# Moving two 32-byte scale tiles from the left to the right end of SBUF in an fp32 encoder-layer kernel

## The chip, the cores and the metric

The kernel runs on one core of a Trainium2 chip. The metric is the device time of one execution in microseconds (us), the median of three runs. Everything said of durations comes from one profiled execution of the kernel before the change.

## The reference

The computation is one layer of a hybrid encoder over two sequences of 1024 tokens with 1024 features each, everything in fp32, and a last normalisation. Cut to what matters:

```python
def layer(x, c, ...):
    mod = silu(c) @ w_ada + b_ada
    sh1, sc1, ga1, sh2, sc2, ga2 = split(mod, 6)
    h = rmsnorm(x, g_mix) * (1.0 + sc1) + sh1
    z = h @ w_in                                  # q_lat 256, kv_lat 128, k_pe 64, f_in 512
    y_mla = mla_group(...)                        # 4 heads, keys 128 + 64 rotary, values 128, softmax
    y_four = fourier_group(f_in, w_four)          # real part of a 2-D FFT over (sequence, 64 channels)
    x = x + ga1 * (concat([y_mla, y_four]) @ w_out)
    h2 = rmsnorm(x, g_ffn) * (1.0 + sc2) + sh2
    return x + ga2 * ((silu(h2 @ w_gate) * (h2 @ w_up)) @ w_down)     # FFN width 2816
# both sequences: y = rmsnorm(layer(x, c), g_final)
```

The two "scale tiles" of the change are `s1`: for each sequence, `g_mix * (1 + sc1)`, the per-feature factor of the first normalisation, as a tile of 128 partitions by 8 floats (32 bytes per partition).

## The kernel before

Every large product is done with three TensorE matmuls in place of one. A helper, `split` (L63 and L64), cuts an fp32 tile into a rounded high part (`fp32r`, ScalarE, L63) and the low rest (VectorE or GpSimd, L64). A helper, `mm3` (L79 to L81), then adds high x high, high x low and low x high into one PSUM bank. So a matmul of the profile at L79, L80 or L81 can belong to any stage; its tile names tell which. After the arrow stands the moving operand first and then the stationary one (`bank<-H,wh`: `H` moves, `wh` stays); `128*128 128x512` means a stationary operand of 128 columns and a moving operand of 512 columns. Loading the stationary operand is an instruction of its own (LDWEIGHTS, engine `PEld`).

The stages, in order of time:

- Modulation vectors, folding of weights and input transposes (about the first 100 us): weights arrive from HBM and PE works on them as they land.
- Input projection and first half of the Fourier mixing (`wz_h`, `wz_l`: 448 columns; `wcs_h`, `wcs_l`: 280 columns for the cosine part, 256 for the sine part; the stationary operands are the tokens, `eoh` and `eol`). In this stage there are 24 special matmuls in a row whose stationary operand `zoc` has only 4 columns.
- Second half of the Fourier mixing (`tb`, `wm`), attention (`ps_s`, `ppt`, `pt`, `gb`, `wv`), and 128-column transposes against an identity (`ident`, `identr`).
- The FFN, from 740 us to the end. Its products are done by a recursive block scheme on 512-column tiles: `H` holds blocks of the normalised input or of the second product, `wh` and `wl` are the split parts of weights or intermediate blocks, and intermediate blocks go through HBM scratch (`s_d`, `t_d`).

All order of work is fixed in the program; the queues of each engine run it as written.

The memory of a partition is filled from two ends. Pools opened without an option stack from the left (low addresses), pools with `side="right"` from the right (high addresses). The pools at the left begin with `const`, which holds, in this order, `ident` and `identr` (512 bytes each), `mhalf`, `cmask`, and eight tiles of 32 bytes: `s1` (two), `sh1`, `s2`, `sh2`. The right stack begins with a pool `edge` whose only tile before the change is one of 104 floats that nothing reads:

```python
edge = ctx.enter_context(tc.tile_pool(name="edge", bufs=1, side="right"))   # L86
edge.tile([P, 104], F32, name="edge")                                        # L87
```

In front of the right pools, another unused tile (`gapz`, 120 floats) makes the pool `zp` a whole multiple of 512 bytes long.

Of the kernel before, what the change touches and what calls it, by code (L numbers as in the profile page):

```python
# [12 lines left out]
F32 = mybir.dt.float32  # L13
# [8 lines left out]
P = 128  # L22
D = 1024
N = 1024
NC = D // P
# [28 lines left out]
def hybrid_encoder_kernel(ctx: ExitStack, tc: tile.TileContext, a: dict):  # L54
# [28 lines left out]
    const = ctx.enter_context(tc.tile_pool(name="const", bufs=1))  # L83
    tiny = ctx.enter_context(tc.tile_pool(name="tiny", bufs=4))
    dram = ctx.enter_context(tc.tile_pool(name="dram", bufs=1, space=DRAM))
    edge = ctx.enter_context(tc.tile_pool(name="edge", bufs=1, side="right"))  # L86
# [37 lines left out]
        nc.vector.tensor_tensor(out=r, in0=w, in1=y, op=ALU.mult)  # L124
        return r

    s1 = [const.tile([P, NC], F32, name=f"s1_{s}") for s in range(2)]
    sh1 = [const.tile([P, NC], F32, name=f"sh1_{s}") for s in range(2)]
    s2 = [const.tile([P, NC], F32, name=f"s2_{s}") for s in range(2)]
    sh2 = [const.tile([P, NC], F32, name=f"sh2_{s}") for s in range(2)]  # L130
# [1097 lines left out]
    with ExitStack() as st:  # L1228
# [117 lines left out]
        for k in range(nit + 4):  # L1346
# [9 lines left out]
            if k < nit:  # L1356
                s, b, h, u = items[k]
# [14 lines left out]
            if 0 <= k - 2 < nit and (k - 2) % 4 == 3:  # L1372
                s, b, h, u = items[k - 2]
# [668 lines left out]
```

## Time and profile before

| what | value |
|---|---|
| time, median of 3 runs | 2016.65 us (2015.29, 2016.65, 2016.70) |
| the profiled execution: its own time, and its span | 2015.8 us, 2015.8 us |
| mean granted TensorE clock | 0.995 |
| PE busy | 1973.1 us, 98% |
| weight loads (PEld) busy, beside PE | 1620.0 us, 80% |
| VectorE (DVE), ScalarE (ACT), GpSimd (POOL) busy | 1390.5, 889.0 and 849.8 us |
| DMA, mean rate over the span | 187 GB/s |

The profile has one row per group of alike instructions: line, engine, operation, output tile, input tiles, shape, count, then busy time and mean duration, then idle time before them with what ended it. Matmuls are pipelined: each is shown as lasting until its last result is out, so neighbours overlap, and what a matmul costs in a stream is the distance from its start to the next one's start, not its duration. That distance is read from the view in order of time, or from a window in which PE never idles: length divided by count.

### The profile page before, as it was taken

The numbers are of one execution on the slowest core, as the hardware profiler recorded it, in microseconds if no ns is written. First come the engines' busy times: TensorE is split into PE (matmuls) and PEld (weight loads), VectorE is DVE, ScalarE is ACT, GpSimd is POOL, SyncE is SP. The second block draws the span as 40 slices with busy tenths as digits, with TensorE's granted clock in tenths as the row PEclk, the third lists the DMA queues.
The fourth block names the chain that finished last, engine by engine and source line by source line (L and its number), as shares of the span: only waits on it lengthen the run. The fifth ranks groups of instructions, "written<-read, shape, count | busy, mean of one in ns | idle before, by whom it ended". The sixth has DMA issues, their size and how long they took to land.

```text
span 2015.8 us, 27568 instructions
## 1 busy us (share of the span) xinstructions
PE 1973.1 (98%) x9526; PEld 1620.0 (80%) x9526; DVE 1390.5 (69%) x2064; ACT 889.0 (44%) x1720; POOL 849.8 (42%) x1012
## 2 busy tenths in 40 slices
PE   6899999999999999999999999999999999999998
PEld 3778778888888877888888888888888888888886
DVE  4557757766687678777777567788755655656784
ACT  2665535555565563333333356453333333335541
POOL 0654312111223237779779410344644554420152
PEclk8999999999999999999999999999999999999999
DMA  9785884445553575645646597665333333267762
GB/s 385 262 318 193 283 331 114 122 94 121 150 123 105 188 256 197 205 158 198 202 155 202 176 314 230 230 229 185 126 99 100 107 103 105 99 203 242 251 228 86
DMA packets 179449, 376.59 MB, mean 187 GB/s; under 512 B 17996, under 2 KB 57548, under 8 KB 175468
## 3 DMA queue, kind: packets, MB, share of 16 engines
q1 hardware_dynamic: 156908, 305.60, 45.3%
q0 software_dynamic: 21824, 68.17, 11.3%
q8 instruction: 75, 1.23, 0.2%
q10 hardware_dynamic: 576, 1.05, 0.1%
q14 instruction: 66, 0.54, 0.1%
HBM read 262.75 MB, written 120.39 MB: 190 GB/s over the span
## 4 chain that ended last, share of the span: by engine, by line
PE 59%; DVE 2%; issue 1%; POOL 1%; ACT 0%; POOLq 0%; DVEq 0%; ACTq 0%
PE bank L80 20%; PE bank L79 20%; PE bank L81 20%; DVE wl L64 1%; DVE val L152 0%; DVE val L1834 0%; DVE H L64 0%; DVE val L1806 0%; POOL rs_y L107 0%; DVE val L149 0%; POOL out_dram L1840 0%; DVE val L1722 0%; POOL rs_w L109 0%; POOL rs_w L110 0%; DVE val L1708 0%
## 5 line engine op out<-in xcount | busy, mean ns | idle before, releaser
L79 PE MATMUL bank<-H,wh 128*128 128x512 f32 x1232 | 480.8, 390 | 3.0 <-DVE val L152 1.3
L80 PE MATMUL bank<-H,wh 128*128 128x512 f32 x1232 | 480.0, 390 | 0.3 <-DVE H L64 0.3
L81 PE MATMUL bank<-H,wl 128*128 128x512 f32 x1232 | 479.8, 390 | 0.2 <-DVE wl L64 0.2
L79 PEld LDWEIGHTS bank<-H,wh 128*128 128x128 f32 x1232 | 231.4, 188 | 53.7 <-DVE val L152 2.6
L64 DVE TENSOR_TENSOR wl<-draw,wh 128x512 fp32r<-128x512 f32 x286 | 208.1, 764 | 90.9 <-ACT wh L63 90.2
L80 PEld LDWEIGHTS bank<-H,wh 128*128 128x128 f32 x1232 | 231.4, 188 | 48.4 <-DVE H L64 0.6
L81 PEld LDWEIGHTS bank<-H,wl 128*128 128x128 f32 x1232 | 231.4, 188 | 48.3 <-DVE wl L64 0.5
L152 DVE TENSOR_TENSOR val<-bank,val 128x512 f32<-128x512 f32 x200 | 136.6, 689 | 162.9 <-PE bank L81 162.3
L63 ACT CAST wh<-draw 128x512 fp32r<-128x512 f32 x286 | 165.1, 619 | 174.2 <-PE bank L80 129.4
L152 POOL TENSOR_TENSOR val<-val 128x512 f32<-128x512 f32 x58 | 81.0, 1398 | 344.2 <-DVE val L1806 164.5
L80 PE MATMUL bank<-wl,wh 128*128 128x512 f32 x572 | 223.3, 390 | 0.9 <-DVE wl L64 0.9
L81 PE MATMUL bank<-wh,wl 128*128 128x512 f32 x572 | 222.8, 390 | 0.0
L79 PE MATMUL bank<-wh 128*128 128x512 f32 x572 | 222.8, 389 | 0.0
L63 ACT CAST wh<-rgu 128x512 fp32r<-128x512 f32 x172 | 107.0, 622 | 257.4 <-PE bank L80 202.7
L63 ACT CAST wh<-val 128x512 fp32r<-128x512 f32 x133 | 82.2, 621 | 262.1 <-PE bank L80 244.9
L64 DVE TENSOR_TENSOR wl<-val,wh 128x512 fp32r<-128x512 f32 x133 | 125.7, 947 | 66.7 <-ACT wh L63 66.7
L64 DVE TENSOR_TENSOR wl<-rgu,wh 128x512 fp32r<-128x512 f32 x172 | 165.4, 961 | 1.4 <-ACT wh L63 1.4
L149 POOL TENSOR_TENSOR val<-rgu 128x512 f32<-128x512 f32 x80 | 107.8, 1347 | 79.4 <-DMA rgu<-in_wgu_dram 75.7
L80 PEld LDWEIGHTS bank<-wl,wh 128*128 128x128 f32 x572 | 107.5, 188 | 24.7 <-DVE wl L64 2.6
L79 PEld LDWEIGHTS bank<-wh 128*128 128x128 f32 x572 | 107.4, 188 | 22.5
L81 PEld LDWEIGHTS bank<-wh,wl 128*128 128x128 f32 x572 | 107.4, 188 | 21.9
L149 POOL TENSOR_TENSOR val<-val 128x512 f32<-128x512 f32 x89 | 119.3, 1358 | 1.3
(400 smaller groups left out, 3897.8 us busy)
## 6 DMA issues: line engine op xcount, KB each, us to landing
rgu<-in_wgu_dram SPq DMA_DIRECT2D x86, 512.0 KB, 4.0
draw<-s_d SPq DMA_DIRECT2D x143, 256.0 KB, 3.3
s_d<-val POOLq DMA_DIRECT2D x88, 256.0 KB, 3.2
draw<-t_d SPq DMA_DIRECT2D x88, 256.0 KB, 4.4
s_d<-val SPq DMA_DIRECT2D x66, 256.0 KB, 3.7
draw<-in_w_down_dram SPq DMA_DIRECT2D x55, 256.0 KB, 4.0
wada<-in_w_ada_dram SPq DMA_DIRECT2D x11, 1024.0 KB, 9.3
xt<-in_x_dram SPq DMA_DIRECT2D x16, 512.0 KB, 10.8
```

Of the source, the lines that this page charges most:

```text
L63: here["a"] = nc.scalar.copy(hi, src).ins
L64: here["v"] = (eng or nc.vector).tensor_tensor(out=lo, in0=src, in1=rd(hi), op=ALU.subtract).ins
L79: nc.tensor.matmul(out, lh, rh, start=first, stop=False, skip_group_check=cont)
L80: nc.tensor.matmul(out, lh, rl, start=False, stop=False, skip_group_check=cont)
L81: here["t"] = nc.tensor.matmul(out, ll, rh, start=False, stop=last, skip_group_check=cont).ins
L149: return eng.tensor_tensor(out=out, in0=x, in1=y, op=ALU.subtract).ins
L152: eng.tensor_tensor(out=out, in0=x, in1=y, op=ALU.add)
```

## The change

`s1` is allocated in the pool `edge` at the right end and not in `const` at the left:

```diff
@@ -124,7 +124,7 @@
-    s1 = [const.tile([P, NC], F32, name=f"s1_{s}") for s in range(2)]
+    s1 = [edge.tile([P, NC], F32, name=f"s1_{s}") for s in range(2)]
     sh1 = [const.tile([P, NC], F32, name=f"sh1_{s}") for s in range(2)]
     s2 = [const.tile([P, NC], F32, name=f"s2_{s}") for s in range(2)]
     sh2 = [const.tile([P, NC], F32, name=f"sh2_{s}") for s in range(2)]
```

The built programs have the same instructions in the same order with the same waits on every engine and queue. What differs is where tiles lie (byte addresses in a partition):

| tile | before | after |
|---|---|---|
| `ident`, `identr`, `mhalf`, `cmask` | 8320, 8832, 9344, 9376 | unchanged |
| `s1_0`, `s1_1` | 9408, 9440 | 229280, 229312 |
| every other tile, left or right | x | x - 64 |

So the distance between any two tiles is kept, except to `s1` and to the four tiles in the first row. Of the 9366 matmul instructions of the program (160 of them, plain fp32, appear twice in the trace, which makes its 9526), by the start address of the operands modulo 512:

| moving operand | stationary operand | matmuls | after |
|---|---|---|---|
| 64 | 64 | 7512 | 0 and 0 |
| 128 (`ident`, `identr`) | 64 | 776 | 128 and 0 |
| 64 | 320 | 236 | 0 and 256 |
| 320 | 320 | 204 | 256 and 256 |
| other pairs, most with a moving operand at some multiple of 32 | | 638 | each 64 less, `ident` and `identr` excepted |

The moving operands at multiples of 32 are those of the Fourier stage: a row of `wcs_h` or `wcs_l` is 536 floats (2144 bytes) long, so that from one of its eight rows (one for each 128 input features) to the next the start moves on by 96 bytes modulo 512, and `wcs_l` lies 256 from `wcs_h`.

## The prediction

> **What bounds the kernel now.** I read the page first, its busy line, its slices and its costliest groups, to see whether one engine is the limit everywhere.
>
> ```profile
> span 2015.8 us, 27568 instructions
> PE 1973.1 (98%) x9526; PEld 1620.0 (80%) x9526; DVE 1390.5 (69%) x2064; ACT 889.0 (44%) x1720; POOL 849.8 (42%) x1012
> PE   6899999999999999999999999999999999999998
> PEclk8999999999999999999999999999999999999999
> ...
> L79 PE MATMUL bank<-H,wh 128*128 128x512 f32 x1232 | 480.8, 390 | 3.0 <-DVE val L152 1.3
> ...
> L80 PE MATMUL bank<-wl,wh 128*128 128x512 f32 x572 | 223.3, 390 | 0.9 <-DVE wl L64 0.9
> ```
>
> PE is full in all but the first slices and the granted clock is at 90% or more from the second slice on (1.00 in the windows below). The two quoted groups stand three times each (L79, L80, L81): 3 x 1232 + 3 x 572 = 5,412 matmuls of 512 columns, with idle time before them of 3.0 us or less per group. So only two things can move the time much: what one matmul costs in the stream, and the few waits. The windows give the first.
>
> ```profile
> core 0: us, PE busy (x), PEclk, DMA share, GB/s
> 1414.00:1957.00 543.00, 543.00 (x2397) 1.00 0.46 151
> 930.00:1320.00 390.00, 390.00 (x1722) 1.00 0.64 213
> ```
>
> In both windows PE never idles and all matmuls have 512 columns. Take one or two off the counts for those cut by the edges: 543/2395.5 = 226.7 ns from start to start. All of these have both operands at 64 modulo 512.
>
> **The change, part by part.** Nothing is added or removed: the order of work, the waits and the queues are kept, and what changes is 64 bytes of start address. The cost is therefore a question of whether a start at 64 costs something that a start at 0 does not.
>
> *Moving operand.* The matmuls at 512 columns are all at 64, so they can't tell. The Fourier stage can, because there the start moves on by 96 bytes from row to row, and in one place the stationary operand has only 4 columns (`zoc`), so its loading is no limit:
>
> ```profile
> start us, us, engine line op out<-in xcount [idle before <-releaser]
> 176.03 0.30 PE L79 MATMUL bank<-wcs_h,zoc 128*4 128x280 f32 x1
> 176.17 0.29 PE L80 MATMUL bank<-wcs_l,zoc 128*4 128x280 f32 x1
> 176.29 0.29 PE L81 MATMUL bank<-wcs_h,zoc 128*4 128x280 f32 x1
> 176.42 0.30 PE L79 MATMUL bank<-wcs_h,zoc 128*4 128x280 f32 x1
> ...
> 176.81 0.30 PE L79 MATMUL bank<-wcs_h,zoc 128*4 128x280 f32 x1
> ...
> 177.20 0.30 PE L79 MATMUL bank<-wcs_h,zoc 128*4 128x280 f32 x1
> ...
> 177.59 0.30 PE L79 MATMUL bank<-wcs_h,zoc 128*4 128x280 f32 x1
> ...
> 177.98 0.30 PE L79 MATMUL bank<-wcs_h,zoc 128*4 128x280 f32 x1
> ...
> 178.37 0.30 PE L79 MATMUL bank<-wcs_h,zoc 128*4 128x280 f32 x1
> ```
>
> Each group of three starts 0.39 us after the one before: 176.03, 176.42, 176.81, 177.20, 177.59, 177.98, 178.37. By the layout, the moving operands of these six groups begin at 160, 256, 352, 448, 32 and 128 modulo 512 (the middle matmul of each at 256 more, so 0 is among them: the second group is 256, 0, 256). Starts at 0, 128 and 256 are as dear as starts at 32 or 96. Per matmul that is 2.34/18 = 130.0 ns. Between 280 and 512 columns the slope is (226.7 - 130.0)/232 = 0.4168 ns a column, which leaves 226.7 - 213.4 = 13.3 ns at either length that don't depend on columns. Since the `zoc` rows carry the same 13.3 ns at every start, I don't read it as a price of the start. I take 0 for the moving operand. The rows are exact to 0.01 us a group, so at most 0.01/3 = 3 ns a matmul; both signs are open.
>
> *Stationary operand.* Where 512 columns stream, the load lies under the matmul before:
>
> ```profile
> 1500.13 0.39 PE L79 MATMUL bank<-H,wh 128*128 128x512 f32 x1
> 1500.36 0.39 PE L80 MATMUL bank<-H,wh 128*128 128x512 f32 x1
> 1500.58 0.39 PE L81 MATMUL bank<-H,wl 128*128 128x512 f32 x1
> 1500.13 0.19 PEld L80 LDWEIGHTS bank<-H,wh 128*128 128x128 f32 x1
> 1500.36 0.19 PEld L81 LDWEIGHTS bank<-H,wl 128*128 128x128 f32 x1
> ```
>
> The load for L80 begins with the matmul L79 at 1500.13 and takes 0.19 us; its own matmul starts at 1500.36, so 0.04 us are spare. A shorter load is worth 0 there; one longer by over 0.04 us (a fifth) would show. Where fewer columns stream, load and stream are both near the limit, and there the trace does show something:
>
> ```profile
> 137.69 0.28 PE L79 MATMUL bank<-wcs_h,eoh 128*128 128x256 f32 x1
> 138.03 0.28 PE L79 MATMUL bank<-wcs_h,eoh 128*128 128x256 f32 x1
> 138.38 0.28 PE L79 MATMUL bank<-wcs_h,eoh 128*128 128x256 f32 x1
> 138.74 0.36 PE L79 MATMUL bank<-wz_h,eoh 128*128 128x448 f32 x1
> ```
>
> The group that begins at 137.69 has its moving operands at 128, 384, 128 and takes 0.34 us; the next two (224, 480, 224 and 320, 64, 320) take 0.35 and 0.36, so 15 ns a group or 5 ns a matmul more. The stationary operand is at 320 in all three. After the change two of the eight rows are again at multiples of 128, others than now, so for these matmuls gain and loss cancel: 0, or up to 24 groups x 15 ns = 0.4 us either way.
>
> *Transposes.* `ident` stays, its partner moves, so their distance changes.
>
> ```profile
> L1271 PE MATMUL ppt<-ident,p 128*128 128x128 f32 x512 | 69.0, 275 | 1.5 <-DVE nb L1252 0.6 <-DVE p L1258 0.3
> L352 PE MATMUL bank<-c,wf 128*128 128x128 f32 x64 | 7.8, 278 | 0.0
> L424 PE MATMUL bank<-ident,xt 128*128 128x128 f32 x32 | 5.1, 322 | 0.0
> ```
>
> The nearest rows with another distance are the 128-column matmuls of `c` and `wf` (both operands moved alike, 278 against 275 ns). So 3 ns x 776 = 2.3 us either way; I take 0, and keep the 322 ns of L424 for the rival below.
>
> *Transfers.* Every SBUF end of a DMA moves by 64 bytes too. Only the start of the kernel waits for DMA:
>
> ```profile
> PE bank L233 <- DMA wide<-in_w_ada_dram: 5.6, 3, 2.5
> PE bank L254 <- DMA wuqT<-in_wuqT_dram: 4.9, 1, 4.9
> PE bank L233 <- DMA wada<-in_w_ada_dram: 3.3, 4, 1.4
> PE bank L269 <- DMA wide<-in_w_out_dram: 2.3, 1, 2.3
> PE bank L1096 <- DMA wada<-in_w_ada_dram: 1.9, 1, 1.9
> 30.00:40.00 10.00, 5.83 (x36) 2.94 (x36) 3.38 (x8) 5.04 (x13) 1.69 (x6) 1.00 1.02 417
> ```
>
> These waits add up to 18.0 us, and in the window from 30 to 40 us the queues are full (share 1.02, 417 GB/s). Their going altogether is the far bound of a gain; nothing in the rows says that a 64-byte shift touches them, so I take 0. The Trainium skill, DMA: Bandwidth & Descriptors, section "How a descriptor splits into AXI transactions", says that a descriptor off a 256-byte boundary also fetches the bytes back to that boundary, in beats of 32 bytes. For rows of 2048 bytes at 64 that would be 66 beats where 64 suffice, an estimate of 3% or 1.5 us on a saturated stretch of some 50 us; no run here shows it, and the sum stands without it.
>
> *Other engines.* DVE, ACT and POOL are at 69% or less; their operands move alike and their cover is the PE stream. Taken as 0. `s1` is read as a per-partition scalar wherever it lies: 0.
>
> **Sum.** 2015.8 + 0 = 2015.8 us for the profiled execution, whose own time is its span. The median of the three runs, 2016.65, is 0.85 us above it; the forecast is put between the two, 2016.3. A change under 0.2% (4 us) can't be told from none here. Its own range, by 2.3 us (transposes), 0.4 us (Fourier rows) and a little from the transfers, is 2012 to 2020.
>
> **The rivals.**
>
> *All of the 13.3 ns is the start address.* Then the 5,412 matmuls above and the 1,732 others of 512 columns (20 groups of which the first and the last are quoted) lose it.
>
> ```profile
> L1242 PE MATMUL ps_s<-lat,qa 128*128 128x512 f32 x128 | 53.6, 419 | 0.7 <-ACT qa L63 0.7
> ...
> L81 PE MATMUL bank<-wm,B 128*128 128x512 f32 x32 | 12.3, 389 | 0.0
> ```
>
> 7,144 x 13.3 ns = 95 us, giving 1921. For it: 64 bytes are 16 floats, and the excess has the size of a few dozen columns. Against it: the `zoc` groups, which pay it at 0 too. The Trainium skill, TensorE: Matmul & The Clock Gate, section "Wait — 56ns, not 53.3ns?", gives N/2.4 + 2.5 ns for back-to-back matmuls, 215.8 ns at 512 columns. The trace has 226.7, so by that rule 10.9 ns a matmul are foreign to it, an estimate of 78 us or 1938 if the address were the cause. Chance 0.06.
>
> *Load and stream disturb each other less from 0.* In the `wcs` rows with 128 stationary columns the group at multiples of 128 was 5 ns a matmul cheaper. If that depends on where the moving operand lies, and not on its distance to the stationary one (which the change keeps), 512-column matmuls gain up to the same: 7,144 x 5 ns = 36 us, 1980; at half of it 1998, at 1 ns 2009. Against it: at 512 columns the load has 0.04 us to spare and the distance of 226.7 ns is the same in both windows. Chance 0.15.
>
> *The transposes get worse* (slower than before). `ident` keeps 128 while its partners go to 0. If the new distance is a bad one, each of 776 transposes pays: by the dearest row, L424, up to 322 - 275 = 47 ns, or 36 us (2053); at 10 ns 2024. It decides beyond 0.2% from 4/776 us = 5 ns each. Against it: in the rows the kind of operand changes with the distance, and L424 lies at the start, where PE waits. A loss of 1 ns on each 512-column matmul (7 us, 2023) I count here. Chance 0.11.
>
> **How the numbers follow.** The forecast has 0.68, of which 0.04 may spill over to faster (transfers) and 0.01 to slower. Faster: 0.06 + 0.15 + 0.04 = 0.25; slower: 0.11 + 0.01 = 0.12; same: 0.63. For 8 in 10 the range takes the forecast's own 2012 to 2020 and reaches to the half-sized gain (1998) and to a loss of 10 ns a transpose (2024); outside are the full gains and the large losses, some 0.17.
>
> **What would show it.** The window from 1414 to 1957 us again with 2397 matmuls or one or two beside (right), or with 2450 and more (5 ns each) or 2540 (13.3 ns each); the `zoc` groups at 0.39 us; L1271 at 275 ns; the waits for DMA at about 18 us. The prediction is wrong if the distance between 512-column matmuls changes by more than 0.5 ns, or if the first 100 us change by more than 4 us.

## The result and the profile after

The changed kernel takes 2012.44 us (median of 20 runs, 2010.8 to 2015.8), the kernel before 2016.76 us (20 runs) beside it. The ratio is 0.998, with a 95% interval of 0.9974 to 0.9987: faster by 4.3 us (2.6 to 5.2 by the interval), right at the 0.2% that I had called the bound of what can be told. All ratios below are against the kernel before on the same chip; a ratio need not be the quotient of the two medians.

The page of the profiled execution of the kernel after (span 2014.0 us, at the upper end of its runs), with the lines that answer to those of the kernel before:

```profile
span 2014.0 us, 27568 instructions
PE 1974.3 (98%) x9526; PEld 1619.1 (80%) x9526; DVE 1392.1 (69%) x2064; ACT 889.1 (44%) x1720; POOL 852.5 (42%) x1012
PE   7899999999999999999999999999999999999998
...
L79 PE MATMUL bank<-H,wh 128*128 128x512 f32 x1232 | 480.7, 390 | 3.2 <-DVE val L152 1.4
```

Its windows in the FFN, with the same columns as before, then three rows of the `zoc` matmuls in order of time, and the transposes in the view by shape:

```profile
1414.00:1957.00 543.00, 542.63 (x2395) 1.00 0.46 151
...
172.77 0.29 PE L79 MATMUL bank<-wcs_h,zoc 128*4 128x280 f32 x1
...
173.16 0.30 PE L79 MATMUL bank<-wcs_h,zoc 128*4 128x280 f32 x1
...
173.55 0.30 PE L79 MATMUL bank<-wcs_h,zoc 128*4 128x280 f32 x1
...
L1271 PE MATMUL ppt<-ident,p 128*128 128x128 f32 x512 | 69.0, 274 | 1.4 <-DVE nb L1252 0.6
```

These matmuls cost the same within a nanosecond: 542.63/2393.5 = 226.7 ns from one 512-column matmul to the next, 0.39 us a `zoc` group (172.77, 173.16, 173.55), 274 ns a transpose against 275. What differs is PE's waiting for transfers:

```profile
PE bank L254 <- DMA wuqT<-in_wuqT_dram: 4.7, 1, 4.7
PE bank L233 <- DMA wide<-in_w_ada_dram: 4.0, 2, 2.4
...
PE bank L233 <- DMA wada<-in_w_ada_dram: 2.2, 2, 1.2
...
PE bank L1096 <- DMA wada<-in_w_ada_dram: 1.7, 1, 1.7
```

These add up to 12.6 us, against 18.0 before. And where the queues are full, they move more. The window from 10 to 50 us, first of the kernel before, then of the kernel after (the columns after the engines are granted clock, DMA share and GB/s):

```profile
10.00:50.00 40.00, 29.78 (x160) 15.75 (x158) 19.14 (x47) 11.67 (x33) 1.74 (x6) 0.87 1.02 413
```

```profile
10.00:50.00 40.00, 32.65 (x163) 16.42 (x158) 18.87 (x47) 11.66 (x33) 1.73 (x6) 0.87 1.02 420
```

The share is 1.02 in both, so the queues are full in both; 420 GB/s against 413 is 1.7% more.

### The profile page after: what moved, and what is told of

It is laid out like the page before. It is cut to its first block, busy times and chain, and to the rows that moved or that the text cites. A ratio compares the mean times of both kernels' runs of the same rounds, so it can differ in the third digit from the quotient of the medians.

```text
span 2014.0 us, 27568 instructions
## 1 busy us (share of the span) xinstructions
PE 1974.3 (98%) x9526; PEld 1619.1 (80%) x9526; DVE 1392.1 (69%) x2064; ACT 889.1 (44%) x1720; POOL 852.5 (42%) x1012
## 4 chain that ended last, share of the span: by engine, by line
PE 57%; DVE 3%; issue 1%; POOL 1%; DMA 1%; ACT 0%; SPq 0%; POOLq 0%; DVEq 0%; ACTq 0%
PE bank L80 19%; PE bank L79 19%; PE bank L81 19%; DVE wl L64 1%; DMA draw<-s_d 1%; DVE val L152 0%; DVE val L1806 0%; DVE val L1834 0%; DVE val L1725 0%; DVE H L64 0%; POOL rs_y L107 0%; ACT wh L63 0%; DVE val L149 0%; POOL out_dram L1840 0%; DVE val L1708 0%
## 5 line engine op out<-in xcount | busy, mean ns | idle before, releaser
L64 DVE TENSOR_TENSOR wl<-val,wh 128x512 fp32r<-128x512 f32 x133 | 131.0, 987 | 67.4 <-ACT wh L63 67.4
```

The lines of the kernel that those rows point to most:

```text
L64: here["v"] = (eng or nc.vector).tensor_tensor(out=lo, in0=src, in1=rd(hi), op=ALU.subtract).ins
```

## Experiments

The theory after the result, T: the gain is in the transfers, because every SBUF end of a DMA now begins on a 256-byte boundary. Its rivals: P, some matmuls got cheaper; L, the place of `s1` itself counts; F, the gain lies in the FFN's transfers and not in those of the start; D (for the kernels with unlike ends), the distance between moving and stationary operand sets what a matmul costs. All kernels compute the same; only the place of tiles differs, by the edits shown, each against the kernel before.

**The change once more** (no edit to the changed kernel):

> The changed kernel once more, all operands and transfer ends at 0 modulo 512. Theory T (the gain is in the transfers at the start, because every SBUF end of a DMA now begins on a 256-byte boundary): 2012 us against 2016.7 before; in the windows from 10 to 60 us the five rates add up to about 2066 GB/s against 2024 in the trace of before; the waits of PE for DMA are some 3 to 5 us shorter; 512-column matmuls stay at 226.7 ns. Theory P (some matmuls got cheaper): the first 110 us are as before and the gain is spread over the stream. Theory N (chance of the runs): 2016.

Measured: 2012.39 us, ratio 0.9978 (0.9968 to 0.9989). The rates from 10 to 60 us are 414, 428, 423, 414 and 385 GB/s, 2064 in sum; 226.8 ns a matmul (542.5/2392.5; the counts of records vary by a few, so 226.7 to 227.0 is one value). PE's waits for DMA are shorter than in the first trace of before by 4.8 us:

```profile
PE bank L254 <- DMA wuqT<-in_wuqT_dram: 4.7, 1, 4.7
PE bank L233 <- DMA wide<-in_w_ada_dram: 4.0, 3, 2.7
PE bank L233 <- DMA wada<-in_w_ada_dram: 2.4, 2, 1.4
PE bank L269 <- DMA wide<-in_w_out_dram: 2.1, 1, 2.1
```

The effect is there again, so N falls; and P with it, since the 512-column matmuls, most of the stream, are no cheaper.

**Another pair of tiles moved:**

```diff
-    s2 = [const.tile([P, NC], F32, name=f"s2_{s}") for s in range(2)]
+    s2 = [edge.tile([P, NC], F32, name=f"s2_{s}") for s in range(2)]
```

> The s2 tiles move to the right end in place of s1, so that the same pools lie at 0 and s1 stays at the left. Theory T and theory P: the same as the changed kernel, 2012 us. Theory L (it is the place of s1 itself, read as a scalar by other engines, that counts): 2016.7 us as before.

Measured: 2013.48 us, ratio 0.9979 (0.9968 to 0.9991). L falls: `s1` is back at the left and the gain is there all the same.

**Left pools at 0, right pools at 64:**

```diff
-    edge.tile([P, 104], F32, name="edge")
+    edge.tile([P, 88], F32, name="edge")
...
-    s1 = [const.tile([P, NC], F32, name=f"s1_{s}") for s in range(2)]
+    s1 = [edge.tile([P, NC], F32, name=f"s1_{s}") for s in range(2)]
```

> The left pools lie at 0 and the right pools at 64, so 585 of the DMA's SBUF ends are on a 256-byte boundary and 486 are not, and the two operands of over 4,000 matmuls lie 64 bytes apart modulo 512. The large loads of the start (x tiles, the modulation weights) are among those at 64. Theory T: between the two kernels, 2014 to 2016.5 us, and the PE stream at 226.7 ns. Theory D (the distance between moving and stationary operand sets what a matmul costs): the windows from 930 to 1320 and from 1414 to 1957 us show another distance than 226.7 ns, by 1 to 5 ns, so 2018 to 2035 us (or as much faster).

Measured: 2039.55 us, ratio 1.0112 (1.0093 to 1.0132), slower than both and beyond what either theory had allowed. The transfers at the start were hardly hurt (419 GB/s from 10 to 50 us, 14.8 us of waits for DMA). The window in the FFN, the groups by shape from 1420 to 1950 us, and the first and the last of ten neighbours in order of time:

```profile
1414.00:1957.00 543.00, 542.50 (x2341) 1.00 0.43 143
...
L80 PE MATMUL bank<-H,wh 128*128 128x512 f32 x569 | 225.0, 395 | 0.0
...
L79 PE MATMUL bank<-wh 128*128 128x512 f32 x194 | 75.5, 389 | 0.0
...
1499.80 0.39 PE L80 MATMUL bank<-H,wh 128*128 128x512 f32 x1
...
1501.90 0.40 PE L80 MATMUL bank<-H,wh 128*128 128x512 f32 x1
```

PE is hardly idle, yet 542.5/2339.5 = 231.9 ns a matmul. The groups with `H` at the left and `wh` at the right last 395 ns, and (1501.90 - 1499.80)/9 = 233 ns lie from one of them to the next; those with both operands at the right last 389 as ever. The instructions, their order and their waits are those of before, and neither 0 nor 64 is dear when both operands share it, so this is the distance: D holds. As a check, the 3 x 1232 matmuls of `H` times 6.6 ns make 24 us, and the kernel is 23 us slower than before.

**All at 192:**

```diff
-    edge.tile([P, 104], F32, name="edge")
+    edge.tile([P, 72], F32, name="edge")
...
+    const.tile([P, 32], F32, name="shift")
```

> All pools lie at 192 modulo 512: no transfer begins on a 256-byte boundary, and it begins further from one than before (64). Theory T with a price that grows with the distance to the boundary below: slower than before, about 2019 to 2021 us, with the rates from 10 to 60 us some 6% under those of before (about 1910 GB/s in sum). That growing price is what the Trainium skill, DMA: Bandwidth & Descriptors, section 'How a descriptor splits into AXI transactions', would give: 70 beats for 2048 bytes at 192, 66 at 64, 64 at 0. Theory T with one price for every start off a boundary: 2016.7 us as before, 2024 GB/s. Theory P with the absolute address: some other time, with another distance between matmuls.

Measured: 2016.48 us, ratio 0.9997 (0.9985 to 1.0008), 226.8 ns a matmul, and in the full queues the rate of before:

```profile
10.00:50.00 40.00, 31.35 (x161) 16.14 (x156) 18.81 (x47) 11.43 (x32) 1.73 (x6) 0.87 1.02 413
```

So a start at 192 is no dearer than one at 64: one price for every start off a boundary. The growing price, as worked out from that section of the Trainium skill, isn't seen here.

**Only the pool p1 at 0, and only the pool p1 at 64.** The first has `s1` in `edge` with a tile of 88 floats, and before the first left pool after p1:

```diff
+    back = ctx.enter_context(tc.tile_pool(name="back", bufs=1))
+    back.tile([P, 16], F32, name="back")
```

> Only the pool p1, the left pool of the first 300 us, lies at 0 modulo 512; all right pools, and all left pools after it, lie at 64 as before. Of the first 26.1 MB that are loaded, 13.7 MB then land on 256-byte boundaries. In the first runs the rates of the windows from 10 to 50 us were those of the changed kernel when just the left pools were at 0 (414, 427, 424, 412 GB/s). Theory T (the transfers of the start): most of the gain, 2013 to 2014.5 us, same rates. Theory F (the transfers of the FFN, which is back at 64 here): 2016.5 us, whatever the rates at the start. The stationary and moving operands of the FFN are both at 64, so 226.7 ns.

The second has `s1` in `edge` with 104 floats, and before the pool p1, closed with it:

```diff
+        off = st.enter_context(tc.tile_pool(name="off", bufs=1))
+        off.tile([P, 16], F32, name="off")
```

> The reverse: only the pool p1 lies at 64 as before, everything else at 0. Theory T: most of the gain gone, 2014.5 to 2016.5 us, rates from 10 to 50 us as before (410, 419, 417, 404). Theory F: the whole gain, 2012.4 us.

Measured, on another chip, where the kernel before took 2018.53 us: 2014.55 us, ratio 0.9982 (0.9974 to 0.9991), and 2014.54 us, ratio 0.9985 (0.9975 to 0.9994). F in its pure form falls, since with the FFN at 64 most of the gain is there. But T, as I had put it, expected the second to lose most of the gain, and it kept over half. Its rates weren't those of before either: 416, 422, 419 and 417 GB/s from 10 to 50 us, 1674 in sum, as high as with p1 alone at 0 (413, 427, 424, 411; 1675). The other 12.4 of the first 26.1 MB, and all later transfers, were on boundaries there. Either half keeps a large part of the gain; the intervals overlap too far to say which is larger. The rates also don't fit a simple price for each transfer off a boundary: with about half of the bytes on one, the sum should lie midway between 1650 and 1679, and it lies at the upper end in both kernels. Why is open.

**All at 256, and left at 0 with right at 256.** The edits are those for 192, with 56 and 48 floats in place of 72 and 32, and those for the right at 64, with 40 floats in place of 88.

> All pools lie at 256 modulo 512. Theory T with a boundary of 256 bytes: the changed kernel's time, 2012.4 us, and its rates (415, 429, 423, 412, 387 GB/s). If the boundary were 512 bytes: 2016.5 us and the rates of before.

> Left pools at 0, right pools at 256: all transfers on 256-byte boundaries, but moving and stationary operand of most FFN matmuls 256 bytes apart. With 64 bytes apart the FFN matmuls had cost 230 to 236 ns in place of 226.7 and the kernel 2039.6 us. Theory D with a period of 256 bytes: 226.7 ns, 2012.4 us. Theory D with a period of 512 or more: another distance between matmuls in the window from 1414 to 1957 us, up to 236 ns (2040 us) or under 226.7 ns (faster than both kernels).

Measured: 2013.57 us, ratio 0.9972 (0.9962 to 0.9983), and 2013.25 us, ratio 0.9973 (0.9963 to 0.9983); rates of 415, 428, 424, 412, 386 and of 416, 428, 421, 415, 374 GB/s; 226.9 ns a matmul in both. A boundary of 256 bytes is as good as 512, and a distance of 256 as good as none. Neither can be told from the changed kernel.

**All at 128, and left at 0 with right at 128.** The edits are those for 192, with 88 and 16 floats in place of 72 and 32, and those for the right at 64, with 72 floats in place of 88.

> All pools at 128 modulo 512. Theory T with a boundary of 256 bytes: the time of before, 2016 to 2018 us, ratio 0.999 to 1.001, rates from 10 to 50 us 1650 in sum. With a boundary of 128 bytes: the changed kernel's, ratio near 0.9975, rates 1679. Moving and stationary operands coincide modulo 256, so 226.7 ns a matmul either way; the transposes now have identity and partner at the same place.

> Left pools at 0, right pools at 128: moving and stationary operand of most FFN matmuls 128 bytes apart. At 64 apart a matmul had cost 230 to 236 ns, at 256 apart 226.7 as at 0. Theory D with a period of 128: 226.7 ns, and 2013 to 2017 us by the transfers. With a period of 256: another distance, 228 to 240 ns and 2025 to 2060 us, or below 226.7 and faster than both kernels.

Measured: 2018.01 us beside 2018.31 of the kernel before, ratio 1.0003 (0.9994 to 1.0013), with the rate of before; and 2038.96 us, ratio 1.0101 (1.0086 to 1.0115). The windows of the two:

```profile
10.00:50.00 40.00, 29.58 (x164) 15.08 (x161) 19.05 (x48) 12.69 (x35) 2.28 (x7) 0.91 1.02 413
```

```profile
1414.00:1957.00 543.00, 542.00 (x2346) 1.00 0.44 144
```

A start at 128 pays the price of a start at 64, so the boundary that counts for transfers is 256 bytes. Operands 128 bytes apart cost 542/2344.5 = 231.2 ns a matmul, so the period of the distance is 256 bytes as well, as far as 64, 128 and 256 bytes tell; 192 was not run.

**Two more traces of the kernel before:**

> The kernel before once more, for a second trace of it. Theory T (the transfers of the start): rates from 10 to 50 us again near 410, 419, 417, 404 (1650 in sum; the kernels at 0 and 256 had 1679 to 1680), PE's waits for DMA near 18 us against 12.6 to 13.8 us, and the 1000th matmul near 195 us against 190.5 to 192.6 us in the kernels at 0 and 256. If its waits are under 14 us, the first trace of before was a slow instance and the start does not carry the gain.

> The same as the look before it: a third trace of the kernel before, to see how far its start varies from run to run.

Measured: spans 2017.1 and 2013.5 us; from 10 to 50 us 414 and 413 GB/s, as in the first trace. The waits for DMA are 16.2 (rows below) and 16.1 us, less than 18.0:

```profile
PE bank L254 <- DMA wuqT<-in_wuqT_dram: 5.8, 1, 5.8
PE bank L233 <- DMA wide<-in_w_ada_dram: 4.1, 2, 3.0
PE bank L269 <- DMA wide<-in_w_out_dram: 2.3, 1, 2.3
PE bank L233 <- DMA wada<-in_w_ada_dram: 2.2, 4, 1.4
PE bank L1096 <- DMA wada<-in_w_ada_dram: 1.8, 1, 1.8
```

The 1000th matmul starts 1.3 and 2.1 us earlier than in the first trace, so one trace is good to some 2 us and the first trace had a slow start. All ten traces whose operands coincide modulo 256, leaving out the two with p1 alone:

| operands and transfers at | ratio | GB/s, 10 to 50 us | PE's waits for DMA, us |
|---|---|---|---|
| 64 (before, three traces) | 1 | 413, 414, 413 | 18.0, 16.2, 16.1 |
| 128 | 1.0003 | 413 | 16.7 |
| 192 | 0.9997 | 413 | 14.2 |
| 0 (the change, again, `s2` moved) | 0.9980, 0.9978, 0.9979 | 420, 420, 420 | 12.6, 13.2, 13.5 |
| 256; 0 and 256 | 0.9972; 0.9973 | 420; 420 | 13.2; 13.8 |

The rates split without overlap, 413 to 414 against 420. The waits split too, though by a hair at 192 (14.2 against 13.8); their means are 16.2 and 13.3 us, 3.0 us apart.

The traces also say where the gain lies. The first matmul of the FFN, the 4043rd of every trace, starts at 756.2 us on average in the five traces off a boundary and at 753.3 in the five on one: 2.8 us earlier, with 2.5 us less idle time of PE before it. Of the 2.8 us, 1.5 are there at the 1000th matmul (near 192 us) and 2.4 at the 1500th (near 279 us). From the FFN's first matmul to the end the traces on a boundary take no less time (1259.7 us against 1258.3), so nothing here puts a gain in the FFN, and F falls once more. What isn't settled is the size: by medians of many runs the gain is 4.3 us, and the mean span of the same ten traces differs by just 1.5 us (2014.5 against 2013.0). Single traces vary too much to close that gap: PE's idle time in the FFN alone goes from 2.5 to 5.0 us.

One rival is left beside T. The mean granted clock of a kernel's runs is 0.9966 to 0.9970 on a boundary and 0.9955 to 0.9963 off it, and on the same chip the two differ by 0.0003 to 0.0011. If all of that counted, it would be 0.6 to 2.2 us of some 2015 us (an estimate). In the traces the clock falls below 1.00 mostly between 10 and 50 us, where PE waits, and there the means of the two groups hardly differ (0.89 and 0.91). So the clock may carry a part of the gain; whether it does, or only follows from shorter waits, no run separates.

## Why the prediction was right or wrong

The time, 2012.44, lies in the range and at the lower end of the forecast's own range (2012 to 2020), but the forecast itself was 2016.3, no change, and that is not what happened: the interval of the ratio ends at 0.9987. That the own range took the time in was partly luck. The terms with a size, 2.3 and 0.4 us, reach from 2013.6 to 2019.0; the rest down to 2012 was "a little from the transfers", which had no size. Of the prediction's signs, those for matmuls came true: 2395 matmuls in the window (2397 before), 0.39 us a `zoc` group, 274 ns a transpose. The first 100 us changed by less than 4 us: the 428th matmul starts at 97.6 us against 99.9. The waits for DMA did not stay at about 18 us, and there the mechanism was missed.

- *Moving operand, 0:* right. The `zoc` groups had told it, and the runs agree: 226.7 to 227.0 ns with all at 0, 64, 128, 192 or 256.
- *Stationary operand, 0:* right for this change, but 0.04 us to spare is no safe reason. The runs with unlike ends show a price in spite of it, 231.2 to 231.9 ns on average at 128 or 64 apart. What makes it 0 here is that moving and stationary operand keep their distance, which the prediction says only in its second rival.
- *Fourier rows, 0:* right in size, but their reading was wrong. The group of 0.34 us, said to be cheap because its moving operands began at multiples of 128, is as cheap after the change, where they begin 64 bytes lower:

```profile
134.80 0.28 PE L79 MATMUL bank<-wcs_h,eoh 128*128 128x256 f32 x1
...
135.14 0.28 PE L79 MATMUL bank<-wcs_h,eoh 128*128 128x256 f32 x1
...
135.50 0.28 PE L79 MATMUL bank<-wcs_h,eoh 128*128 128x256 f32 x1
```

By the median of the eight such runs of groups it takes 348 ns before and 349 after, and the two behind it 357 and 356 both times. So the differences belong to the place in the run of groups and not to the start address.
- *Transposes, 0:* right. They are at 274 ns with identity and partner 128 apart modulo 256, at 275 with 64, and at 274 where they coincide (all at 128), so for these 128-column matmuls the distance makes no difference.
- *Transfers, 0:* this is the step that failed, a term of the sum taken as nothing. The gain is 4.3 us by medians, and PE's waits for DMA fell from 16.2 to 13.3 us on average. I had the waits (18.0 us as the far bound) and the full queues (share 1.02), and still wrote that nothing in the rows says that a 64-byte shift touches them. That was so: no row of before had a transfer on a 256-byte boundary beside it to compare. Where a resource is full and its price can't be bounded by a row, 0 was the end of the range and not its middle.
- *The estimate of 1.5 us*, worked out from the Trainium skill, DMA: Bandwidth & Descriptors, section "How a descriptor splits into AXI transactions" (3% of 50 us), had the sign, and the boundary of 256 bytes, which the runs at 0, 128, 192 and 256 confirm. The section speaks of bytes that are fetched, though, and the SBUF end of a load is written. The gain in the full queues was 1.7%, not 3%, and the price didn't grow with the distance to the boundary. PE's waits shrank by 3.0 us and not by the 0.7 us that 1.7% of 40 us make. A part may come from later full stretches: from 220 to 240 us the share is 1.00 and 1.02 in the kernel before, and the wait at L1096 (1.9 us) lies there, so that not only the start waits for DMA, as I had written. That the waits shrank is shown, not why by so much; a later start of each load that waits for its buffer would be one way, and it was not tried.
- *The rivals:* the 13.3 ns per matmul stayed at every start, so the first falls. The second, that load and stream disturb each other less from 0, falls in its absolute form, while its other half (they disturb each other by their distance) is shown. The third, worse transposes, didn't occur. Its dearest row was misread as well: the 322 ns of L424 are the mean of two kinds, as its own view tells (shortest, median and longest in ns):

```profile
L424 PE MATMUL bank<-ident,xt x32: 272/273/422, 47.5 to 68.7; 128*128 128x128 f32 x32
```

The mean is 321 ns after the change, and 273 with all at 256, where the places modulo 256 are those after the change; the granted clock from 40 to 50 us is 0.66 before, 0.83 after and 1.00 with all at 256. So the slow ones go with a lowered clock and not with an address. A slower side there is, but not in this change: 21 to 23 us for operands that lie 128 or 64 bytes apart.

## What to carry to other kernels

Look where both operands of a matmul lie before looking where either lies: here any common place modulo 256 bytes gave the same 226.7 ns for 512-column matmuls, and places 64 or 128 bytes apart cost 1% of the kernel. Then put the common place on a 256-byte boundary, which here cost two moved tiles and brought 1.7% of the rate where the queues are full. When a full resource is touched and no row prices the touch, give it the sign that a mechanism suggests and not zero.

## What the runs showed of the hardware that I had not expected

- A matmul of 512 fp32r columns takes 226.7 ns from start to start if moving and stationary operand begin at the same place modulo 256 bytes, and longer at the two other distances run: with `H` at 0 and `wh` at 64 it takes 233 ns, and its duration is 395 ns against 389, though in the kernel before the load of the stationary operand had 0.04 us to spare. No wait shows it; it is seen only in the count per window (2341 against 2397).
- In full queues, which held mostly loads into SBUF, the rate was 420 GB/s with every SBUF end on a 256-byte boundary, 413 to 414 with all of them 64, 128 or 192 bytes past one, and 419 with about half of the bytes on one.
- The price of a start off a boundary is flat, and it shows in the rate of a window sooner than in the time: 1.7% of the rate repeated in every trace, where the spans of three traces of the kernel before differ by 3.6 us (2013.5 to 2017.1).
